# A hybrid attention block: the scan's second operand in PSUM, and dilated queries copied by residue

## The chip, the cores and the metric

The kernel runs on one core of one Trainium2 chip. A core has five engines that run side by side: TensorE (PE, matrix products; its weight loads are shown as PEld), VectorE (DVE), ScalarE (ACT), GpSimd (POOL) and SyncE (SP), which here issues the DMAs. PE reads its operands from SBUF and writes to PSUM, which has eight banks of 128 x 512 floats. Each engine works through its own queue in order and waits on semaphores for the others. The metric is the device time of one execution in microseconds (us), the median of the runs.

## The reference

One layer of a decoder, sequence 1024, width 1024, everything float32. The heads fall into two groups of eight (64 wide). Group A ("dilated") uses normalised, rotated q and k and a softmax over a strided window for three window and stride pairs; group B ("stick-breaking") has no softmax. Cut to what matters here:

```python
DILATED_PAIRS = ((128, 1), (512, 4), (2048, 16))   # (window, dilation)

# group A: every query t attends t, t-r, t-2r, ..., t-window for each (window, r);
# the three results are weighted by their softmax denominators

# group B, one block of 128 queries against all keys, strictly causal
z = jnp.einsum('bhqd,bhkd->bhqk', qblk, k) * scale
log_beta = jax.nn.log_sigmoid(z)
log_keep = jnp.where(causal, jax.nn.log_sigmoid(-z), 0.0)
suffix = lax.cumsum(log_keep, axis=3, reverse=True) - log_keep
a = jnp.where(causal, jnp.exp(log_beta + suffix), 0.0)
out = jnp.einsum('bhqk,bhkd->bhqd', a, v)

# then
mixed = concat(rmsnorm(o_A), rmsnorm(o_B))
x = x + mixed @ w_out
x = x + (silu(h @ w_gate) * (h @ w_up)) @ w_down,  h = rmsnorm(x)
```

## The kernel before

The program is straight-line code; a scheduler puts the instructions of each engine in an order from a simulated timeline, and allots the buffers of each tag in the order in which the program asks for them. Products are exact to float32 by splitting one or both factors into a high and a low part, so most products are two or three matmuls (`mm3`).

The stages, in order: the norm of x and the projection of v for group A; q and k for group A with norm and rotation (`rope_norm`), written to DRAM; the attention of the eight head pairs; the output projection; the feed-forward part, from about 650 us to the end, whose products follow a seven-product scheme (lines 884 to 1110). The change concerns the attention.

A *pair* is two heads, stored one above the other in the 128 partitions. Pairs 0 to 3 are group A, 4 to 7 group B. `prep` gets a pair's operands ready while the pair before it is attended: `set_k` and `set_q` write `kh`, `kl` (high and low part of k) and `qs` (q, high part in one half of the partitions, low part in the other, one tile for each head s). `more()` issues background work between the steps, metered by `LEAD`, `PRE` and `RATES`: the projections of the later pairs (`project`, tile pp), and then `merge_a`, group A's share of the output projection (tile yo). `hold` ties the background matmuls to the score matmul `gate[0]` that stands before them in the program.

Group A, `attend_a` (589): two halves hf of 512 queries, four blocks k in each, and for each block two kinds of unit (`unit_a`, 407). The near unit (lay 0) has 128 neighbouring queries against up to 256 neighbouring keys. The dilated unit (lay 1) has the 128 queries of one residue mod 4 in the half, against the keys of that residue, which `set_k` stores together. Its q is taken by a stride:

```python
if lay:
    n = 128 * hf + 128
    q, keys = slice(512 * hf + k, 512 * hf + 512, 4), lambda t: t[:, 256 * k:256 * k + n]
```

In both kinds q is the matmul's weights (420, 421) and the keys stream past. DVE adds a mask and takes the row's extreme (422), ACT the exponential (424). Some units later `turn_a` (461) turns the result on PE (469), `evac` (502) copies it out, and PE multiplies it by v (478) into an accumulator: near in the PSUM tag "t", dilated in "pv"; ACT copies both out at the end of a half (483). `factors` and `finish` weigh the two kinds, through small DMAs and POOL products (585, 586).

Group B, `attend_b` (611): for each block of 128 queries and each head, `unit_b` (517) makes the scores (401 to 404), ACT two sigmoids into kp and p (522), DVE a running product of kp backward (525), and POOL for one head, DVE for the other, the product of p with it (526). The scan is

```python
nc.vector.tensor_tensor_scan(rv, rv, rv, 1.0, op0=ALU.mult, op1=ALU.bypass)
```

whose second operation is a bypass, so its second input does not count; here it is kp once more. `ptpv` (529) turns the result (542) and multiplies by v (551). Buffers: kp has two (tag "G"), the scores two PSUM banks ("s").

PSUM tags and their banks: "d" 2, "t" 1, "s" 2, "pt" 2, "pv" 1. `out_rstd` (647) makes the output's norm from sums of squares that PE adds up in a small tile ssp: in tag "t", but in "d" for the last one. Its squares are gathered in `acc`, one tile of 128 x 1024 (705, 757). The output tiles reloaded for it (`load_o`, 642) are in tag "qr", as the rotated q and k were before.

Of the kernel before, what the change touches and what calls it, by code (L numbers as in the profile page):

```python
# [11 lines left out]
F32 = mybir.dt.float32  # L12
FR = mybir.dt.float32r
AF = mybir.ActivationFunctionType
ALU = mybir.AluOpType
# [17 lines left out]
def f(ap):  # L33
    return ap.bitcast(F32)
# [3 lines left out]
def tile_hybrid_block(ctx, tc, x, attn_norm_w, w_in, q_norm_w, k_norm_w, dil_w, sb_w,  # L38
# [276 lines left out]
    def set_q(pr, hf, p):  # L315
        sl = slice(hf * 512, hf * 512 + 512)
        for s in range(2):
            a, b = slice(64 * s, 64 * s + 64), slice(64 - 64 * s, 128 - 64 * s)
            nc.scalar.activation(pr.qs[s][a, sl], p[a, :], AF.Copy)
            nc.vector.tensor_tensor(pr.qs[s][b, sl], p[a, :], f(pr.qs[s][a, sl]), op=ALU.subtract)  # L320

    def set_k(pr, hf, p):

        def half(t):
            return t.rearrange("p (c w) -> p c w", c=4)[:, :, 128 * hf:128 * hf + 128]

        p = p.rearrange("p (c w) -> p c w", c=4)
        for s in range(2):
            a, b = slice(64 * s, 64 * s + 64), slice(64 - 64 * s, 128 - 64 * s)
            kh, kl = half(pr.kh[s]), half(pr.kl[s])  # L330
            nc.scalar.activation(kh[a], p[a], AF.Copy)
            nc.scalar.activation(kh[b], p[a], AF.Copy)
            nc.vector.tensor_tensor(kl[a], p[a], f(kh[a]), op=ALU.subtract)
# [24 lines left out]
    def back(qr):  # L358
        p = PS.tile([128, 512], F32, "pt", "bk")
        for k in range(4):  # L360
            nc.tensor.transpose(p[:, k * 128:(k + 1) * 128], qr[:, k, :], ident)
        return p

    def prep(pr, g, i):

        pr.ot, pr.g, pr.i = [None, None], g, i
        head_tiles(pr, i)
        if g == 0:
            for which, put in ((1, set_k), (0, set_q)):
                for hf in range(2):  # L370
                    t = att.tile([128, 4, 128], F32, tag="rl", name="rl", bufs=3)
                    nc.sync.dma_start(t, qk[which][hf * 512:hf * 512 + 512, 128 * i:128 * i + 128].rearrange(("(t p) e -> p t e", "(p t) e -> p t e")[which], t=4))
                    put(pr, hf, back(t))
                    yield 0.9
            for hf in range(2):
                set_va(pr, hf, i)
            yield 0.1
        else:
            todo = [(1, hf, s, 0.3) for hf in range(2) for s in range(2)] + [(which, hf, None, 0.6) for which in (0, 2) for hf in range(2)]
            there = []  # L380
            for n, (which, hf, s, cost) in enumerate(todo):
                while len(there) < min(n + 3, len(todo)):
                    w, h, one, _ = todo[len(there)]
                    while (1, i, w, h) not in ready:
                        more()
                    there.append(load_raw(1, i, w, h, one))
                t = there[n]
                if which == 1:
                    set_kb(pr, hf, s, t)
                else:  # L390
                    (set_q, None, set_v)[which](pr, hf, t)
                yield cost
# [14 lines left out]
    def unit_a(pr, s, lay, k, hf, p, nm, den):  # L407


        if lay:  # L410
            n = 128 * hf + 128
            q, keys = slice(512 * hf + k, 512 * hf + 512, 4), lambda t: t[:, 256 * k:256 * k + n]
        else:
            c = 512 * hf + 128 * k
            n = 256 if c else 128
            q, w = slice(c, c + 128), (c + 128 - n) // 4

            keys = lambda t: t.rearrange("p (c w) -> p c w", c=4)[:, :, w:w + n // 4].rearrange("p c (b u) -> p b c u", u=32)
        sp = PS.tile([128, 512], F32, "s", "sc")[:, :n]
        gate[0] = nc.tensor.matmul(sp, pr.qs[s][:, q], keys(pr.kh[s]), start=True, stop=False)  # L420
        nc.tensor.matmul(sp, pr.qs[s][:, q], keys(pr.kl[s]), start=False, stop=True)  # L421
        nc.vector.tensor_tensor_reduce(p[:, :n], sp, mask[:, lay, 256 - n:256], scale=-0.125, scalar=3.0e38,  # L422
                                       op0=ALU.add, op1=ALU.min, accum_out=nm)
        last_exp[0] = nc.scalar.activation(p[:, :n], p[:, :n], AF.Exp, bias=nm, scale=-1.0, accum_out=den)
# [92 lines left out]
    def unit_b(pr, s, qb, tag):  # L517
        n = (qb + 1) * 128
        p, kp = P4("pb", tag), P4("kp", "G")
        for sp, c0, c1 in scores(pr, s, qb):  # L520
            for t, scale in ((kp, -0.125), (p, 0.125)):
                i = nc.scalar.activation(t[:, c0:c1], sp, AF.Sigmoid, scale=scale)  # L522
                after(i, last_exp[0], "one activation table at a time")
        rv = kp[:, n - 1::-1] if n == 1024 else kp[:, :n][:, ::-1]
        nc.vector.tensor_tensor_scan(rv, rv, rv, 1.0, op0=ALU.mult, op1=ALU.bypass)  # L525
        (nc.gpsimd, nc.vector)[s].tensor_tensor(p[:, :n - 1], p[:, :n - 1], kp[:, 1:n], op=ALU.mult)  # L526
        return p

# [60 lines left out]
    def attend_a(pr, o):  # L589

        pr.acc, pr.o = [None, None], [[None, None], [None, None]]
        for hf in range(2):
            p = []
            st = att.tile([128, 2, 4, 2, 2], F32, tag="st", name="st", bufs=2)
            for k in range(4):
                p.append(P4("pa"))
                for lay in range(2):
                    n = 128 * hf + 128 if lay else 256 if hf or k else 128
                    for s in range(2):
                        c = 512 * lay + 256 * s + (0 if lay else 256 - n)  # L600
                        unit_a(pr, s, lay, k, hf, p[k][:, c:c + n], st[:, lay, k, 0, s:s + 1], st[:, lay, k, 1, s:s + 1])
                    catch_up(2 if len(pend) > 2 else 1)
                    yield 1.5
                for items in far(pr, hf, k) + near(pr, hf, k):
                    pend.append((now[0], lambda items=items, p=p, hf=hf: turn_a(pr, hf, p, items)))
            weigh, wide = factors(st)
            wait = WEIGH + (2 if hf and pr.i == 3 else 0)
            chores.append((now[0] + wait, weigh))
            chores.append((now[0] + wait + USE, lambda hf=hf, wide=wide: finish(pr, hf, o, wide)))

    def attend_b(pr, o):

        late = None
        for g in range(4):
            pq = []
            for k in range(2):
                pq.append([unit_b(pr, s, 2 * g + k, "PPPE"[2 * k + s]) for s in range(2)])
                catch_up(2)
                yield 0.2 * (2 * g + k + 1)
            if late:  # L620
                while pend:
                    catch_up(9)
                ptpv(*late)
                yield 0.92 * (2 * late[1] + 1.5)
            late = (pr, g, pq, o)
        ptpv(*late)
        yield 0.92 * (2 * late[1] + 1.5)
# [18 lines left out]

    def out_rstd(g, hf, acc):

        ssp = PS.tile([128, 4], F32, "d" if g and hf else "t", "ssp")
        for k in range(4):  # L650
            nc.tensor.matmul(ssp[:, k:k + 1], acc[hf][:, k * 128:(k + 1) * 128], ones, start=True, stop=True)
        r = big.tile([128, 4], F32, name="rg%d%d" % (g, hf))
        nc.vector.tensor_scalar(r, ssp, 1.0 / 512, EPS, op0=ALU.mult, op1=ALU.add)
        nc.gpsimd.tensor_tensor(r, r, mhalf[:, :4], op=ALU.pow)
        return r
# [44 lines left out]
    def merge_a():  # L700
        for tt in range(4):
            t = H("x2", F32)
            x2.append(t)
        parts = [[H("oh"), H("ol")] for hf in range(2)]
        t = att.tile([128, 1024], F32, tag="acc", name="acc", bufs=1)
        acc = [t[:, 0:512], t[:, 512:1024]]
        for hf in range(2):
            for tt in (2 * hf, 2 * hf + 1):
                nc.sync.dma_start(x2[tt].rearrange("p (a c) n -> p a (c n)", a=2),
                                  x[tt * 256:(tt + 1) * 256, :].rearrange("(a p) d -> p a d", p=128))  # L710
            yield from merge(0, hf, parts, acc)
# [42 lines left out]
        more()  # L754

    parts = [[H("oh"), H("ol")] for hf in range(2)]
    t = att.tile([128, 1024], F32, tag="acc", name="acc", bufs=1)
    acc = [t[:, 0:512], t[:, 512:1024]]
    for _ in merge(1, 0, parts, acc):
        pass  # L760
    tail = merge(1, 1, parts, acc)
# [256 lines left out]
    sums = [H("tk", F32) for _ in range(4)]  # L1018
    right_sum = [t[:, k, :] for t in sums[:3] for k in range(4)]
    left_sum = [sums[3][:, k, :] for k in range(4)]  # L1020
    for tag, n in (("k2", 2), ("k2", 2), ("acc", 1), ("kh", 4)):
        t = att.tile([128, 1024], F32, tag=tag, name="lk", bufs=n)
        left_sum += [t[:, 0:512], t[:, 512:1024]]

# [129 lines left out]
```

## Time and profile before

| | us |
|---|---|
| median of 3 runs | 1328.32 |
| lowest, highest | 1328.2, 1330.47 |
| the profiled execution's own time | 1330.71 |
| its span (first to last instruction) | 1328.9 |

The mean granted clock of TensorE was 0.986 of full speed in the profiled execution. How to read its rows: a row of the line view has the line in the code, the engine, the operation, the tile written and those read, how often, and then the durations in ns (least, median, most). A row of the groups has busy time in us, the mean of one in ns and the idle time of the engine in front of it with what ended it. A row of the timeline has start and length in us; matmuls are pipelined, so their lengths overlap, and the distance from start to start tells what one costs. A row of the waits has the sum in us, how often, and the longest. A row of the windows has from and to, the length, busy time and instructions of PE, PEld, DVE, ACT and POOL, then the granted clock, the share of time that the DMA engines were busy, and GB/s. The chain is the row of instructions that ended last, each held up by the one before it.

### The profile page before, as it was taken

The numbers are of one execution on the slowest core, as the hardware profiler recorded it, in microseconds if no ns is written. First come the engines' busy times: TensorE is split into PE (matmuls) and PEld (weight loads), VectorE is DVE, ScalarE is ACT, GpSimd is POOL, SyncE is SP. The second block draws the span as 40 slices with busy tenths as digits, with TensorE's granted clock in tenths as the row PEclk, the third lists the DMA queues.
The fourth block names the chain that finished last, engine by engine and source line by source line (L and its number), as shares of the span: only waits on it lengthen the run. The fifth ranks groups of instructions, "written<-read, shape, count | busy, mean of one in ns | idle before, by whom it ended". The sixth has DMA issues, their size and how long they took to land.

```text
span 1328.9 us, 18238 instructions
## 1 busy us (share of the span) xinstructions
PE 1286.0 (97%) x6260; PEld 1019.1 (77%) x6260; DVE 857.2 (65%) x1407; ACT 624.1 (47%) x1305; POOL 387.3 (29%) x318
## 2 busy tenths in 40 slices
PE   7999999999978978999999999999999999999998
PEld 6888887777756755767888888888888887788886
DVE  4224345556478767794779677666546777985775
ACT  6331266776676867664555222233332323344442
POOL 6388701211224325243312222222222321010000
PEclk9999999999989999999999999999999999999999
DMA  9533133554323143122326654422546448502642
GB/s 279 208 111 103 72 113 104 127 139 114 107 86 113 61 154 135 56 79 81 103 68 213 187 167 135 142 88 79 151 136 198 122 150 302 165 30 97 197 137 86
DMA packets 189324, 172.58 MB, mean 130 GB/s; under 512 B 33712, under 2 KB 134192, under 8 KB 189232
## 3 DMA queue, kind: packets, MB, share of 16 engines
q1 hardware_dynamic: 189232, 171.42, 41.6%
q8 instruction: 49, 0.80, 0.3%
q14 instruction: 43, 0.35, 0.1%
HBM read 133.96 MB, written 37.42 MB: 129 GB/s over the span
## 4 chain that ended last, share of the span: by engine, by line
PE 85%; DVE 4%; ACT 4%; DMA 4%; issue 2%; POOL 1%; SPq 0%; DVEq 0%; ACTq 0%; POOLq 0%
PE yd L1054 14%; PE gu L94 11%; PE gu L95 11%; PE gu L91 11%; PE va L95 3%; PE va L91 3%; PE va L94 3%; PE pp L91 3%; PE pp L94 3%; PE pp L95 3%; PE pv L551 2%; PE yo L94 2%; PE yo L91 2%; PE yo L95 2%; PE pv L478 2%
## 5 line engine op out<-in xcount | busy, mean ns | idle before, releaser
L829 ACT ACTIVATE wh<-wr 128x512 fp32r<-128x512 f32 x132 | 83.2, 631 | 209.1 <-PE gu L94 163.2
L94 PE MATMUL gu<-t,wh 128*128 128x512 f32 x352 | 139.0, 395 | 0.0
L91 PE MATMUL gu<-t,wh 128*128 128x512 f32 x352 | 138.8, 394 | 0.0
L95 PE MATMUL gu<-t,wl 128*128 128x512 f32 x352 | 138.8, 394 | 0.0
L525 DVE TENSOR_TENSOR_SCAN kp<-kp 128x128 f32<-128x128 f32 (+7 forms) x64 | 108.5, 1706 | 28.1 <-ACT kp L522 26.4
L1054 PE MATMUL yd<-dl,dh 128*128 128x512 f32 x308 | 122.4, 397 | 3.1 <-DVE dl L830 2.9
L1054 PE MATMUL yd<-dh,dl 128*128 128x512 f32 x308 | 121.6, 395 | 0.0
L94 PE MATMUL gu<-b,wh 128*128 128x512 f32 x264 | 104.5, 396 | 0.0
L91 PE MATMUL gu<-b,wh 128*128 128x512 f32 x264 | 104.3, 396 | 0.0
L95 PE MATMUL gu<-b,wl 128*128 128x512 f32 x264 | 104.2, 396 | 0.0
L830 DVE TENSOR_TENSOR wl<-wr,wh 128x512 fp32r<-128x512 f32 x105 | 80.6, 767 | 7.8 <-ACT wh L829 7.7
L1054 PE MATMUL yd<-dh 128*128 128x512 f32 x308 | 85.5, 398 | 0.0
L526 POOL TENSOR_TENSOR pb<-pb,kp 128x127 f32<-128x127 f32 (+7 forms) x32 | 43.0, 1345 | 128.5 <-DVE kp L525 54.7
L422 DVE CUSTOM_DVE_ANT_0 pa<-sc,mask 128x256 f32<-128x256 f32 (+1 forms) x128 | 46.3, 380 | 50.6 <-PE sc L421 49.6
L95 PE MATMUL va<-wt,hl 128*128 128x512 f32 x192 | 76.4, 401 | 2.6 <-DVE hl L62 2.6
L91 PE MATMUL va<-wt,hh 128*128 128x512 f32 x192 | 76.6, 405 | 1.9 <-ACT hh L61 1.9
L91 PEld LDWEIGHTS gu<-t,wh 128*128 128x128 f32 x352 | 66.2, 188 | 15.8
L91 PE MATMUL pp<-hh,wh 128*128 128x512 f32 x192 | 78.2, 408 | 0.0
L94 PEld LDWEIGHTS gu<-t,wh 128*128 128x128 f32 x352 | 66.2, 188 | 15.7
L95 PEld LDWEIGHTS gu<-t,wl 128*128 128x128 f32 x352 | 66.1, 188 | 15.6
L829 ACT ACTIVATE dh<-wd 128x512 fp32r<-128x512 f32 x55 | 34.8, 632 | 91.3 <-PE yd L1054 84.5
L94 PE MATMUL va<-wt,hh 128*128 128x512 f32 x192 | 76.4, 400 | 0.0
(208 smaller groups left out, 3166.0 us busy)
## 6 DMA issues: line engine op xcount, KB each, us to landing
wd<-in_w_down_dram SPq DMA_DIRECT2D x88, 256.0 KB, 2.8
wr<-in_w_gate_dram SPq DMA_DIRECT2D x80, 256.0 KB, 3.0
wr<-in_w_up_dram SPq DMA_DIRECT2D x60, 256.0 KB, 3.1
raw<-in_w_in_dram SPq DMA_DIRECT2D x48, 256.0 KB, 4.0
raw<-in_w_out_dram SPq DMA_DIRECT2D x32, 256.0 KB, 2.9
raw<-rq SPq DMA_DIRECT2D x24, 256.0 KB, 2.5
g<-gu SPq DMA_DIRECT2D x20, 256.0 KB, 5.9
xt<-in_x_dram SPq DMA_DIRECT2D x8, 512.0 KB, 6.9
```

What stands on the lines that cost most here:

```text
L91: i = nc.tensor.matmul(ps, a[0], b[0], start=first, stop=False)
L94: nc.tensor.matmul(ps, a[0], b[1], start=False, stop=False)
L95: return nc.tensor.matmul(ps, a[1], b[0], start=False, stop=last)
L422: nc.vector.tensor_tensor_reduce(p[:, :n], sp, mask[:, lay, 256 - n:256], scale=-0.125, scalar=3.0e38, op0=ALU.add, op1=ALU.min, accum_out=nm)
L478: nc.tensor.matmul(pr.acc[lay][64 * s:64 * s + 64, cols], v[:, 64 * s:64 * s + 64], th[:, c:c + n], start=first, stop=last)
L525: nc.vector.tensor_tensor_scan(rv, rv, rv, 1.0, op0=ALU.mult, op1=ALU.bypass)
L526: (nc.gpsimd, nc.vector)[s].tensor_tensor(p[:, :n - 1], p[:, :n - 1], kp[:, 1:n], op=ALU.mult)
L551: i = nc.tensor.matmul(pr.pv[64 * s:64 * s + 64, c - n:c], pr.v[:, j, 64 * s:64 * s + 64], th[:, n * s:n * s + n], start=j == 0, stop=j == ...
L829: nc.scalar.activation(h, r, AF.Copy)
L830: two(n).tensor_tensor(l, r, f(h), op=ALU.subtract)
L1054: mm = nc.tensor.matmul(pp[k], a[x][:, c], b[y], start=not more and j == 0 and x + y == 0, stop=j == HF - 1 and x == 1, skip_group_check=True)
```

## The change

Two edits and what they need. First, `by_residue` copies each half of q on POOL into a tile qf in which the four residues stand one after another, and the dilated unit takes a contiguous block of it as weights. The first half is copied in `prep`, the second at the start of `attend_a`. The tiles are in tags "acc" (head 0) and "qr" (head 1), two buffers each; `acc` becomes two tiles of 512 columns for that. Second, the scan's bypassed input becomes one column of zeros in PSUM, spread over all columns by a step of zero. It lies in the one bank of tag "t" for the whole of group B, so that the sums of squares (ssp) move from "t" to "d".

```diff
+    def by_residue(pr, hf):
+
+        for s in range(2):
+            t = att.tile([128, 512], FR, tag=("acc", "qr")[s], name="qf", bufs=2)
+            nc.gpsimd.tensor_copy(t.rearrange("p (c w) -> p c w", c=4), f(pr.qs[s][:, hf * 512:hf * 512 + 512]).rearrange("p (w c) -> p c w", c=4))
+            pr.qf[hf].append(t)
...
     def prep(pr, g, i):
-        pr.ot, pr.g, pr.i = [None, None], g, i
+        pr.ot, pr.g, pr.i, pr.qf = [None, None], g, i, [[], []]
...
                     put(pr, hf, back(t))
+                    if which == 0 and hf == 0:
+                        by_residue(pr, 0)
                     yield 0.9
...
         if lay:
             n = 128 * hf + 128
-            q, keys = slice(512 * hf + k, 512 * hf + 512, 4), lambda t: t[:, 256 * k:256 * k + n]
+            q, keys = pr.qf[hf][s][:, 128 * k:128 * k + 128], lambda t: t[:, 256 * k:256 * k + n]
         else:
...
-            q, w = slice(c, c + 128), (c + 128 - n) // 4
+            q, w = pr.qs[s][:, c:c + 128], (c + 128 - n) // 4
...
-        gate[0] = nc.tensor.matmul(sp, pr.qs[s][:, q], keys(pr.kh[s]), start=True, stop=False)
-        nc.tensor.matmul(sp, pr.qs[s][:, q], keys(pr.kl[s]), start=False, stop=True)
+        gate[0] = nc.tensor.matmul(sp, q, keys(pr.kh[s]), start=True, stop=False)
+        nc.tensor.matmul(sp, q, keys(pr.kl[s]), start=False, stop=True)
...
-        nc.vector.tensor_tensor_scan(rv, rv, rv, 1.0, op0=ALU.mult, op1=ALU.bypass)
+        nc.vector.tensor_tensor_scan(rv, rv, aside[0][:, 0:1].to_broadcast([128, n]), 1.0, op0=ALU.mult, op1=ALU.bypass)
...
     def attend_a(pr, o):
         pr.acc, pr.o = [None, None], [[None, None], [None, None]]
+        by_residue(pr, 1)
...
+    aside = [None]
     def attend_b(pr, o):
+        if aside[0] is None:
+            aside[0] = PS.tile([128, 512], F32, "t", "aside")
+            nc.vector.memset(aside[0][:, 0:1], 0.0)
...
     def out_rstd(g, hf, acc):
-        ssp = PS.tile([128, 4], F32, "d" if g and hf else "t", "ssp")
+        ssp = PS.tile([128, 4], F32, "d", "ssp")
...
-    t = att.tile([128, 1024], F32, tag="acc", name="acc", bufs=1)
-    acc = [t[:, 0:512], t[:, 512:1024]]
+    acc = [att.tile([128, 512], F32, tag="acc", name="acc", bufs=2) for _ in range(2)]
...
+    left_sum += [att.tile([128, 512], F32, tag="acc", name="lk", bufs=2) for _ in range(2)]
-    for tag, n in (("k2", 2), ("k2", 2), ("acc", 1), ("kh", 4)):
+    for tag, n in (("k2", 2), ("k2", 2), ("kh", 4)):
```

More of the change, by code (lines that the diff above doesn't have):

```diff
@@ L756, in tile_hybrid_block @@
     parts = [[H("oh"), H("ol")] for hf in range(2)]
-    t = att.tile([128, 1024], F32, tag="acc", name="acc", bufs=1)
-    acc = [t[:, 0:512], t[:, 512:1024]]
+    acc = [att.tile([128, 512], F32, tag="acc", name="acc", bufs=2) for _ in range(2)]
     for _ in merge(1, 0, parts, acc):
```

## The prediction

> **What bounds the kernel now.** I read the page first, then the windows by stage, then the PE timeline inside the dilated stage, then the waits and the chain inside the stick-breaking stage. The page gives the span:
>
> ```profile
> span 1328.9 us, 18238 instructions
> ```
>
> The change touches two stages only: the dilated attention (lines 420 to 424, about 176 to 363 us) and the stick-breaking attention (lines 401 to 526, about 363 to 590 us). The windows view, with PE, PEld, DVE, ACT and POOL busy time and then the granted clock:
>
> ```profile
> 176.00:363.00 187.00, 186.23 (x1162) 146.88 (x1161) 99.12 (x387) 131.87 (x382) 35.99 (x28) 1.00 0.43 114
> 363.00:590.00 227.00, 200.02 (x1154) 146.97 (x1153) 176.15 (x155) 161.34 (x353) 84.73 (x53) 0.94 0.29 93
> ```
>
> The reader sees two different limits. In the first stage PE is busy 186.23 of 187 us at full clock: anything that PE stops doing there shortens the stage until ACT (131.87) is the next limit. In the second PE is idle for 227 − 200.0 = 27 us, its clock falls to 0.94, and DVE is busy 176 us: something in the DVE, ACT and POOL chain holds PE up at times, but DVE too is idle for 51 us, so it isn't a plain DVE bound.
>
> **Part 1: q as contiguous weights.** The line view of L420 and four pairs of rows from the PE timeline. Each pair is the first matmul of four (two heads, each against kh and kl) and a background matmul behind it:
>
> ```profile
> L420 PEld LDWEIGHTS sc<-kh,qs x128: 186/250/334, 177.4 to 359.6; 128*128 128x128 f32 x128
> ```
>
> ```profile
> 256.83 0.48 PE L420 MATMUL sc<-kh,qs 128*128 128x256 f32 x1
> ...
> 257.85 0.40 PE L91 MATMUL pp<-hh,wh 128*128 128x512 f32 x1
> ...
> 260.33 0.36 PE L420 MATMUL sc<-kh,qs 128*128 128x256 f32 x1
> ...
> 260.89 0.40 PE L91 MATMUL pp<-hh,wh 128*128 128x512 f32 x1
> ```
>
> ```profile
> 226.34 0.23 PE L420 MATMUL sc<-kh,qs 128*128 128x128 f32 x1
> ...
> 227.38 0.39 PE L94 MATMUL pp<-hl,wh 128*128 128x512 f32 x1
> ...
> 177.60 0.22 PE L420 MATMUL sc<-kh,qs 128*128 128x128 f32 x1
> ...
> 178.28 0.40 PE L94 MATMUL pp<-hl,wh 128*128 128x512 f32 x1
> ```
>
> The weight loads come in two kinds, 186 to 334 ns. Units alternate between near (contiguous q) and dilated (every fourth q). With 256 keys, the slow four take 257.85 − 256.83 = 1.02 us and the fast four 260.89 − 260.33 = 0.56: 0.46 apart, for equal moving sizes. With 128 keys I measure to the second background matmul, because the slow load delays the first one as well: 227.38 − 226.34 = 1.04 against 178.28 − 177.60 = 0.68, 0.36 apart. The keys of the slow units are the contiguous ones, so it is the strided q as weights that costs.
>
> L420 runs 128 times: 64 near, 64 dilated, that is 32 dilated fours, 16 with 128 keys and 16 with 256. Sum: 16 × 0.46 + 16 × 0.36 = **13.1 us** of PE time, in a stage where PE has 0.8 us to spare. The most would be 32 × 0.46 = 14.7. The least is 0, if another chain takes its place; ACT has 55 us idle there and DVE 88, and the scores are turned and multiplied several units later, so I take all of it.
>
> The Trainium skill, "SBUF — State Buffer", section "Door 1: The DMA port swizzle", in its note on 16-byte cachelines, says that accesses that each cross to a new line pay, yet also that fp32 may be strided by 4 for free. Its second half speaks against this edit, since q's step is 4 floats; by it the sum would lose the 13.1 and leave about 1322. The loads of 334 beside 186 ns side with the first half.
>
> What it adds: 16 POOL copies (4 pairs × 2 halves × 2 heads) of 128x512 with a strided read. No such copy is in the trace; the nearest rows are
>
> ```profile
> L308 POOL MEMSET kl<- 64x1024 f32 x4 | 3.7, 946 | 12.2 <-PE ptr L109 12.2
> L665 POOL TENSOR_TENSOR wo<-raw,wo 128x512 fp32r<-128x512 f32 x16 | 27.2, 1709 | 20.0 <-ACT wo L664 12.9 <-issue 6.8
> ```
>
> a write of 1024 columns and a contended two-input operation of the same size. So 0.5 to 1.7 us; I take 1.2, between them, some 19 us on a POOL that is busy 36 of 187. Cover: the first half is copied a pair ahead, the second at the pair's start, eight half-steps (some 20 us) before its first reader. Only the first pair is short of it, worth 1 to 2 us at most, and background projections are queued there. In POOL's queue nothing behind a copy is urgent, and a copy sits behind no wait long enough to use up the slack. I cost it at 0; without the cover it is two copies, 2.4 us, per half. No DMA is added or moved. That qf shares the tags of acc and of the reloaded outputs holds back loads and squares that now run early, with a whole stage to spare: 0.
>
> **Part 2: the scans.** The page's group of all 64 scans, two scans with nothing beside them, and a POOL product:
>
> ```profile
> L525 DVE TENSOR_TENSOR_SCAN kp<-kp 128x128 f32<-128x128 f32 (+7 forms) x64 | 108.5, 1706 | 28.1 <-ACT kp L522 26.4
> ```
>
> ```profile
> 364.21 0.42 DVE L525 TENSOR_TENSOR_SCAN kp<-kp 128x128 f32<-128x128 f32 x1 [1.15 <-ACT kp L522]
> 571.75 2.02 DVE L525 TENSOR_TENSOR_SCAN kp<-kp 128x896 f32<-128x896 f32 x1
> 509.41 1.54 POOL L526 TENSOR_TENSOR pb<-pb,kp 128x767 f32<-128x767 f32 x1 [8.57 <-DVE kp L525]
> ```
>
> From 0.42 at 128 columns and 2.02 at 896 a scan costs 0.153 + 2.083 ns a column. Eight sizes (128 to 1024), eight of each, are 36,864 columns: 76.8 + 64 × 0.153 = 86.6 us. Measured are 108.5, so 21.9 us aren't the scan's own. The next rows tell where they are; first the chain, then the same scans with their sizes:
>
> ```profile
> 509.93 2.65 DVE kp L525
> 519.33 3.11 DVE kp L525
> 566.52 3.13 DVE kp L525
> 583.63 4.08 DVE kp L525
> ```
>
> ```profile
> 509.93 2.64 DVE L525 TENSOR_TENSOR_SCAN kp<-kp 128x768 f32<-128x768 f32 x1 [0.69 <-ACT kp L522]
> 519.33 3.10 DVE L525 TENSOR_TENSOR_SCAN kp<-kp 128x896 f32<-128x896 f32 x1
> 566.52 3.13 DVE L525 TENSOR_TENSOR_SCAN kp<-kp 128x768 f32<-128x768 f32 x1 [0.20 <-ACT kp L522]
> 583.63 4.08 DVE L525 TENSOR_TENSOR_SCAN kp<-kp 128x1024 f32<-128x1024 f32 x1
> ```
>
> The second head's scan starts while POOL multiplies the first head's. The scan at 509.93 finds POOL at work from 509.41 to 510.95, 1.02 us more, and takes 2.64 where its own time is 1.75: 0.89 longer. It all but waits POOL out. Would an operand in PSUM avoid it? Two rows of plain operations of 512 columns:
>
> ```profile
> L865 DVE TENSOR_TENSOR u<-gu,u 128x512 f32<-128x512 f32 x54 | 37.0, 685 | 21.2 <-PE gu L95 20.2 <-DMA u<-early 0.9
> L830 DVE TENSOR_TENSOR t<-t,t 128x512 fp32r<-128x512 f32 x16 | 10.9, 680 | 0.0
> ```
>
> With a PSUM operand 685 ns, with both in SBUF and POOL out of the way 680. So PSUM costs nothing per column and I take 86.6 for the scans. The Trainium skill, "SBUF — State Buffer", section "Who interferes with whom", says a Vector instruction with two SBUF inputs and a GpSimd one that reads SBUF lock each other out for a whole instruction, and with one SBUF input don't; by it the sum is the same 21.9, and the stretched scans agree.
>
> How much reaches the end? Scans on the chain: 0.89 + 1.09 + 1.37 + (4.08 − 2.28) = **5.2 us** that go with the lock. PE's idle 27 us also lower its clock: 0.06 × 227 = 13.6 us lost, of which 5.2/27 comes back, 2.6. Together **7.8**. Least 0 (the rest of the chain, exponentials and DMA, is late next), most 21.9 + 13.6, held by the 27 + 13.6 that PE has to give. The waits say why I stay low; of PE's two longest only the second is the scans' own:
>
> ```profile
> PE sc L401 <- ACT pb L522: 7.8, 7, 3.8
> PE pt L542 <- DVE pb L526: 6.5, 7, 1.5
> ACT qs L319 <- DMA rl<-raw: 11.4, 3, 4.4
> ```
>
> **Part 3: the PSUM bank.** The operand is a column of bank "t", which also holds the near accumulator of the dilated stage. Its memset, and so the first scan, must wait for that accumulator's last copy:
>
> ```profile
> 369.22 0.63 ACT L338 ACTIVATE kh<-rl 128x512 fp32r<-128x512 f32 x1 [3.55 <-DMA rl<-raw]
> ...
> 375.12 0.61 ACT L483 ACTIVATE o<-pv 128x512 f32<-128x512 f32 x1
> ```
>
> The first scan moves from 364.21 to about 375.8, 11.5 us. Behind it wait POOL's and DVE's products, then the sigmoids of the next block, as kp has two buffers, and the scores behind them. But ACT, in whose queue the second block's sigmoids stand, waited for a DMA until 369.22, so that block was late as it is, and without its sigmoids in front the copy comes sooner. So 0 to 11.5; I take **+2**, nearer the small end, as that stall hides most of it. The norm sums that leave "t" for "d" (two buffers): each takes a "d" buffer for one small DVE read while one product fills the other, 0.
>
> **Sum.** −13.1 − 7.8 + 2 = −18.9. The profiled execution took 1330.7 us, 1.8 around its span; it becomes 1311.8. It lies 2.4 above the median of the runs, so the median becomes 1328.3 − 18.9 = **1309**. Its own range is 1300 to 1317.
>
> **The rivals.**
> - **The second stage gives nothing back**: the bank's wait costs up to 11 and the freed DVE time waits for DMA and ACT. For it: the 11.4 us that ACT waits for q's loads; against it: the locked scans on the chain. 1328.3 − 13.1 + 0 to 6: 1315 to 1322. Chance 0.18.
> - **The second stage is freed wholly**: 21.9 of scans and most of the clock: 1328.3 − 13.1 − 13 to 27, 1288 to 1302. For it: DVE is its busiest helper; against: the first wait row, whose longest piece is a DMA's. Chance 0.12.
> - **Part 1 doesn't do what it says**: stride isn't what slows the load, or ACT becomes late at once. Then −7.8 + 2: 1322. Against it: 186 and 334 ns alternate with the units. Chance 0.05.
> - **Slower**: the scan reads PSUM by a slower path, at 3 cycles a column and not 2. That adds 36,864 × 1.04 = 38.4: scans of 125.0, 16.5 above now, all on the path at worst: −13.1 + 2 + 16.5, 1334. It turns slower from a mean scan of (108.5 + 11.1)/64 = 1.87 us. Against it: 685 beside 680 ns. Chance 0.05.
>
> **How the numbers follow.** The forecast has 0.57; the last 0.03 is no visible change. Faster by over 0.2% (about what a measurement of this kernel can tell from none, 2.7 us): 0.57 + 0.18 + 0.12 + 0.05, cut to 0.90 for the overlap with the bank's cost; same 0.05; slower 0.05. The range runs from the middle of the second rival to the end of the first, 1296 to 1322.
>
> **What would show it.** Right: all L420 loads near 190 ns, dilated fours of 0.56 us, the first stage near 174 us with PE still full; 64 scans at 86 to 88 us whatever POOL does; the first scan some 10 us behind the first sigmoid; the second stage 4 to 8 us shorter. Wrong: dilated matmuls that wait for POOL's qf, scans above 1.4 us in the mean, or a new idle stretch of PE between the stages that is longer than 6 us.

## The result and the profile after

The median went from 1328.26 us (1326.69 to 1330.47) to 1310.05 us (1308.62 to 1310.73), 18.2 us less. The measured ratio, which is not the quotient of these medians (0.9863), is 0.9853 [0.9839, 0.9867], or 19.5 us less. The profiled execution of the changed kernel took 1310.01 us; its span is 20.7 us shorter than that of before. The mean granted clock rose from 0.986 to 0.990. First the page of the changed kernel:

```profile
span 1308.2 us, 18283 instructions
```

Then its windows: group A's stage, cut 12 us earlier than before, as group B's first scores come 12.4 us earlier; the 220 us behind it; and the 30 us around the seam between them. After the three columns of time come PE, PEld, DVE, ACT and POOL, then the granted clock, DMA share and GB/s:

```profile
176.00:351.00 175.00, 172.36 (x1163) 131.93 (x1162) 101.21 (x386) 128.74 (x380) 50.08 (x40) 1.00 0.45 118
351.00:571.00 220.00, 195.19 (x1157) 143.41 (x1156) 160.64 (x162) 162.98 (x359) 69.29 (x53) 0.96 0.32 103
346.00:376.00 30.00, 20.18 (x118) 14.94 (x117) 18.86 (x30) 17.85 (x41) 8.40 (x8) 0.77 0.42 117
```

PE is still nearly full in group A's stage, but 2.6 us are idle where 0.8 were. In group B PE is idle for 24.8 of 220 us, where it was 27 of 227, at a clock of 0.96 in place of 0.94. Of that idle time 9.8 us lie in the third row, at the seam, where PE's clock was 0.77.

The view of one line, the scores of group A, shows the weight loads (PEld) and what they waited for:

```profile
L429 PEld LDWEIGHTS sc<-kh,qs x64: 186/188/192, 177.0 to 345.1; 128*128 128x128 f32 x64
...
L429 PEld LDWEIGHTS sc<-kh,qf x64: 186/190/217, 180.1 to 347.5; 128*128 128x128 f32 x64
...
  POOL qf L326: 1.0, 1
```

The two kinds of load have become one. The copies were waited for once, for 1.0 us. The page's group of the scans:

```profile
L534 DVE TENSOR_TENSOR_SCAN kp<-kp,aside 128x128 f32<-128x128 f32 (+7 forms) x64 | 85.4, 1347 | 29.2 <-ACT kp L531 28.9
```

108.5 us have become 85.4, where 86.6 were worked out as the scans' own time. The timeline of one microsecond shows a scan beside POOL's product:

```profile
393.04 1.78 POOL L535 TENSOR_TENSOR pb<-pb,kp 128x895 f32<-128x895 f32 x1 [6.48 <-PE pt L551]
...
393.51 2.02 DVE L534 TENSOR_TENSOR_SCAN kp<-kp,aside 128x896 f32<-128x896 f32 x1 [0.64 <-ACT kp L531]
```

POOL works until 394.82, so for 1.31 us of the scan's 2.02, and 2.02 us is what 896 columns took before with nothing beside them.

**Where the time came from.** Three stretches can be cut out of the two stages by the first and last matmuls of three lines. For group B the rows are, of the kernel before and then of the changed one:

```profile
L401 PE MATMUL sc<-kh,qs x96: 220/446/775, 361.6 to 579.3; 128*128 128x512 f32 x48, 128*128 128x128 f32 x16, 128*128 128x256 f32 x16, 128*128 128x384 f32 x16
...
L551 PE MATMUL pv<-th,v x320: 272/379/688, 381.7 to 613.1; 128*64 128x256 f32 x128, 128*64 128x128 f32 x32
```

```profile
L410 PE MATMUL sc<-kh,qs x96: 220/442/775, 349.2 to 558.6; 128*128 128x512 f32 x48, 128*128 128x128 f32 x16, 128*128 128x256 f32 x16, 128*128 128x384 f32 x16
...
L560 PE MATMUL pv<-th,v x320: 272/379/689, 374.6 to 591.5; 128*64 128x256 f32 x128, 128*64 128x128 f32 x32
```

"A" is the time from group A's first score to its last, "start of B" from group B's first score to its first product with v, "rest of B" from there to the last score. In us, for the profiled execution of each kernel that is spoken of below:

| kernel | A | start of B | rest of B |
|---|---|---|---|
| before | 182.1 | 361.6 to 381.7: 20.1 | to 579.3: 197.6 |
| after | 170.3 | 349.2 to 374.6: 25.4 | to 558.6: 184.0 |
| after, once more on another chip | 170.4 | 25.3 | 187.1 |
| part 1 alone | 172.7 | 25.4 | 195.5 |
| part 2 alone | 184.1 | 22.2 | 185.8 |
| copies made but not read | 182.8 | 21.5 | 196.9 |
| bank taken later | 170.7 | 23.5 | 183.7 |
| scan with a zero in SBUF | 170.9 | 24.4 | 193.4 |
| loads later | 173.1 | 16.2 | 193.8 |
| loads and bank later | 171.0 | 13.2 | 192.4 |

The change gained 11.8 us in A and 13.6 in the rest of B, and gave back 5.3 at the start of B. The second profile of the same kernel has 3.1 us more in the rest of B, and the kernel whose copies nobody reads has 1.4 more at the start than the kernel before: differences of this size between single profiles carry no meaning. Background work that PE does sooner or later can shift time between the last two columns as well.

### The profile page after: what moved, and what is told of

It reads as the page before. It is cut to its first block, busy times and chain, and to the rows that moved or that the text cites. A ratio compares the mean times of both kernels' runs of the same rounds, so it can differ in the third digit from the quotient of the medians.

```text
span 1308.2 us, 18283 instructions
## 1 busy us (share of the span) xinstructions
PE 1264.8 (97%) x6260; PEld 998.6 (76%) x6260; DVE 839.7 (64%) x1408; ACT 621.4 (47%) x1305; POOL 390.3 (30%) x334
## 4 chain that ended last, share of the span: by engine, by line
PE 87%; DMA 4%; ACT 3%; DVE 3%; issue 2%; SPq 0%; POOL 0%; DVEq 0%; ACTq 0%; POOLq 0%
PE yd L1069 14%; PE gu L94 11%; PE gu L95 11%; PE gu L91 11%; PE va L95 3%; PE va L91 3%; PE va L94 3%; PE pp L91 3%; PE pp L94 3%; PE pp L95 3%; PE pv L560 2%; PE yo L91 2%; PE pv L487 2%; PE yo L95 2%; PE yo L94 2%; PE pt L551 2%
## 5 line engine op out<-in xcount | busy, mean ns | idle before, releaser
L534 DVE TENSOR_TENSOR_SCAN kp<-kp,aside 128x128 f32<-128x128 f32 (+7 forms) x64 | 85.4, 1347 | 29.2 <-ACT kp L531 28.9
L95 PE MATMUL pp<-hh,wl 128*128 128x512 f32 x192 | 76.0, 396 | 0.0
L94 PE MATMUL pp<-hl,wh 128*128 128x512 f32 x192 | 75.6, 394 | 0.0
```

The lines of the kernel that those rows point to most:

```text
L94: nc.tensor.matmul(ps, a[0], b[1], start=False, stop=False)
L95: return nc.tensor.matmul(ps, a[1], b[0], start=False, stop=last)
L534: nc.vector.tensor_tensor_scan(rv, rv, aside[0][:, 0:1].to_broadcast([128, n]), 1.0, op0=ALU.mult, op1=ALU.bypass)
```

## The experiments

Ratios are against the kernel before on the same chip, whose median there was 1331 to 1332 us; "x us" is one minus the ratio, times 1328.3. Here too a ratio need not be the quotient of the medians: for part 2 alone that would be 0.9929, or 9.5 us less, beside 0.9941.

**Each part alone.** The first kernel has the copies and nothing of the scan's edit; the second is the kernel before with the scan's edit.

```diff
 # part 1 alone
-        nc.vector.tensor_tensor_scan(rv, rv, aside[0][:, 0:1].to_broadcast([128, n]), 1.0, op0=ALU.mult, op1=ALU.bypass)
+        nc.vector.tensor_tensor_scan(rv, rv, rv, 1.0, op0=ALU.mult, op1=ALU.bypass)
 # part 2 alone
-            q, keys = pr.qf[hf][s][:, 128 * k:128 * k + 128], lambda t: t[:, 256 * k:256 * k + n]
+            q, keys = slice(512 * hf + k, 512 * hf + 512, 4), lambda t: t[:, 256 * k:256 * k + n]
```

> Only the contiguous copy of q; the scans read kp twice as before, no bank is held, and ssp is back in tag t. The theory of the prediction: 13.1 us less than before, 1315 us, with all dilated weight loads near 190 ns, scans at 108 us in sum, and the first scan about 4 us behind the first sigmoid or earlier. By the trace of the changed kernel, in which the last dilated unit came 12 us earlier: 1316. The rival that the dilated stage only moves the waits into the next stage (the DMA loads at the seam of the stages don't get shorter): 1320 to 1325.

> Only the scan's second input in PSUM, with the bank held from the start of group B and ssp in tag d; q is strided as before. By the prediction's terms -7.8 + 2: 1322.5 us. By the trace of the changed kernel, where group B is about 14 us shorter behind its start and its start about 5 us longer: -9, 1319. Both expect scans of 85 to 87 us in sum. The rival that the two parts need each other (the scans' gain shows only when PE is freed before): 1326 to 1330.

Part 1 alone: 1321.49 us, 0.9919 [0.9893, 0.9945], 10.8 us less. Part 2 alone: 1322.27 us, 0.9941 [0.9924, 0.9958], 7.8 us less. Together that is 18.6, and the change as a whole took off 17.9 to 19.5 (0.9865 [0.9849, 0.9881] on another chip, 0.9853 above): the parts add up. The table says where each acts. Part 1 takes 9.4 us out of A and puts 5.3 into the start of B, where no bank was held: that loss belongs to part 1, and with it part 1 lands where the rival of its expectation stood (1320 to 1325), not at 1315. Part 2 takes 11.8 us out of the rest of B and puts 2.1 into its start. The groups of the scans, of part 1 alone and of part 2 alone:

```profile
L534 DVE TENSOR_TENSOR_SCAN kp<-kp 128x128 f32<-128x128 f32 (+7 forms) x64 | 108.9, 1712 | 28.5 <-ACT kp L531 26.8
```

```profile
L525 DVE TENSOR_TENSOR_SCAN kp<-kp,aside 128x128 f32<-128x128 f32 (+7 forms) x64 | 85.4, 1348 | 30.6 <-ACT kp L522 30.5
```

**The copies alone.** Part 1 has a cost (POOL's copies, the shared buffers) and a gain (contiguous weights). This kernel makes the copies and doesn't read them.

```diff
-            q, keys = pr.qf[hf][s][:, 128 * k:128 * k + 128], lambda t: t[:, 256 * k:256 * k + n]
+            q, keys = pr.qs[s][:, 512 * hf + k:512 * hf + 512:4], lambda t: t[:, 256 * k:256 * k + n]
...
-        nc.vector.tensor_tensor_scan(rv, rv, aside[0][:, 0:1].to_broadcast([128, n]), 1.0, op0=ALU.mult, op1=ALU.bypass)
+        nc.vector.tensor_tensor_scan(rv, rv, rv, 1.0, op0=ALU.mult, op1=ALU.bypass)
```

> The kernel before with the 16 POOL copies of q by residue and their tiles, which nothing reads: the units take their strided q and the scans read kp twice. It prices what part 1 adds. The prediction costs the copies at 0: within 2 us of the kernel before. The rival that the copies cost on their way (POOL's queue, POOL's reads against DVE, the tags of acc and of the reloaded outputs): 3 to 6 us slower, which would be the difference between the 13 us predicted for part 1 and the 8 to 11 measured.

1331.05 us, 0.9997 [0.9987, 1.0007]. The copies are there, 18.3 us of POOL by the line view, and cost nothing that shows:

```profile
L326 POOL CAST qf<-qs 128x512 fp32r<-128x512 f32 x16 | 18.3, 1148 | 35.3 <-DVE qs L320 35.0 <-POOL qf L326 0.3
```

**A step of two floats.** The copy keeps two residues side by side, so that the weights have a step of 8 bytes in place of 16 (before) or 4 (after).

```diff
-            nc.gpsimd.tensor_copy(t.rearrange("p (c w) -> p c w", c=4), f(pr.qs[s][:, hf * 512:hf * 512 + 512]).rearrange("p (w c) -> p c w", c=4))
+            nc.gpsimd.tensor_copy(t.rearrange("p (d w c) -> p d w c", d=2, c=2), f(pr.qs[s][:, hf * 512:hf * 512 + 512]).rearrange("p (w d c) -> p d w c", d=2, c=2))
...
-            q, keys = pr.qf[hf][s][:, 128 * k:128 * k + 128], lambda t: t[:, 256 * k:256 * k + n]
+            q, keys = pr.qf[hf][s][:, 256 * (k // 2) + k % 2:256 * (k // 2) + 256:2], lambda t: t[:, 256 * k:256 * k + n]
```

> The changed kernel, but the copy keeps two residues side by side, so that the dilated weights have a step of 2 floats (8 bytes) in place of 1; before it was 4 (16 bytes). If what counts is whether two reads fall into one 16-byte piece: loads near 190 ns and 1310 us. If every step above 1 costs: loads between 190 and 334 ns and up to 13 us more.

The view of line 429, and the line view's group of the copies:

```profile
L429 PEld LDWEIGHTS sc<-kh,qf x64: 192/197/337, 181.2 to 352.1; 128*128 128x128 f32 x64
```

```profile
L326 POOL CAST qf<-qs 128x512 fp32r<-128x512 f32 x16 | 11.2, 707 | 32.5 <-DVE qs L320 29.8 <-PE sc L430 1.7 <-POOL qf L326 0.8
```

The median load is 197 ns, near the 188 of contiguous weights and far from the slow kind, 0.31 to 0.33 us: of the steps tried here, 8 bytes cost next to nothing and 16 bytes do. Of the 128 loads of this line and the next, two are above 250 ns, both where the granted clock was 0.66. The copies became shorter, 707 ns for the 1148 above. The one execution took 1319.79 us, where 1310 was expected; PE's granted clock was 0.66 in it from 316 to 326 us, which nothing here ties to the edit, so its time isn't read.

**A second operand in SBUF that isn't kp.** Is the slow scan one that reads kp twice, or one that has two operands in SBUF? Here the bypassed input is a column of zeros in SBUF, and no bank is taken.

```diff
-        nc.vector.tensor_tensor_scan(rv, rv, aside[0][:, 0:1].to_broadcast([128, n]), 1.0, op0=ALU.mult, op1=ALU.bypass)
+        nc.vector.tensor_tensor_scan(rv, rv, zero.to_broadcast([128, n]), 1.0, op0=ALU.mult, op1=ALU.bypass)
```

> The changed kernel, but the scan's bypassed input is a column of zeros in SBUF, spread by a step of zero, and no bank is held. If it is POOL's reads that lengthen a scan with two inputs in SBUF: scans of 105 to 109 us in sum, long ones beside a POOL product, 1314 to 1317 us as the kernel with the copy of q alone. The rival that the scan is slow because it reads the tile it overwrites a second time: scans of 86 us and a time of 1305 to 1308, for want of a bank's wait.

1324.81 us, 0.9953 [0.9935, 0.9971], above the 1314 to 1317 expected; its ten runs lie between 1321.24 and 1334.25, and part 1 alone, at 0.9919, isn't told from it. The group of its scans:

```profile
L534 DVE TENSOR_TENSOR_SCAN kp<-kp,zero 128x128 f32<-128x128 f32 (+7 forms) x64 | 107.6, 1692 | 27.4 <-ACT kp L531 25.5
```

107.6 us, as before the change: one address, read over and over for a result that doesn't use it, is enough, if it lies in SBUF. What counts is where the operand lies, not that kp is read twice.

**POOL's product taken away.** In the kernel before, DVE multiplies for both heads.

```diff
-        (nc.gpsimd, nc.vector)[s].tensor_tensor(p[:, :n - 1], p[:, :n - 1], kp[:, 1:n], op=ALU.mult)
+        nc.vector.tensor_tensor(p[:, :n - 1], p[:, :n - 1], kp[:, 1:n], op=ALU.mult)
```

> The kernel before, but the products of p with the scanned kp are all on DVE, so that POOL no longer works beside the second head's scan; the scans still have both inputs in SBUF. If POOL's work lengthens them: most of the 22 us goes, scans of 88 to 96 us in sum (POOL's other products, of weights and of the group-A outputs, still fall beside some), with some 30 us more products on DVE. If a scan with both inputs in SBUF is slow by itself: 105 to 109 us again.

The scans with two operands in SBUF, by the page's groups:

```profile
L525 DVE TENSOR_TENSOR_SCAN kp<-kp 128x128 f32<-128x128 f32 (+7 forms) x64 | 91.7, 1437 | 22.3 <-ACT kp L522 22.0
```

16.8 of the 21.9 us are gone with POOL's product. The timeline tells where the rest is, if each scan is set against its own time, 0.153 us + 2.083 ns a column, as worked out in the prediction. The 51 scans that have no POOL work beside them are 0.1 us above it in sum, the 13 others 5.3 us. These 5.3 us lie on scans that found POOL already at work, on the sums of squares (640) or on the low part of the output weights (665). A scan that came first kept its own time, though POOL then worked on the weights (74) or weighed an output (585). One of each, 384 columns behind POOL and 896 columns ahead of it:

```profile
551.18 1.45 POOL L665 TENSOR_TENSOR wo<-raw,wo 128x512 fp32r<-128x512 f32 x1 [0.24 <-ACT wo L664]
551.42 2.02 DVE L525 TENSOR_TENSOR_SCAN kp<-kp 128x384 f32<-128x384 f32 x1
...
401.70 2.02 DVE L525 TENSOR_TENSOR_SCAN kp<-kp 128x896 f32<-128x896 f32 x1
402.22 2.56 POOL L74 TENSOR_TENSOR wl<-raw,wh 128x512 fp32r<-128x512 f32 x1 [24.47 <-ACT wh L72]
```

The first took 2.02 us where its own time is 0.95. By the same count for the kernel before, 23 scans found POOL already at work and are 22.5 us above their own time in sum. The 41 others, with POOL idle or starting behind them, are 0.4 us below theirs. In the changed kernel 23 scans found POOL at work too, and none is longer than its own time. The one execution took 1326.74 us beside 1331.15 of the kernel before, with 32 products more for DVE; a single run says no more than that.

**The bank taken later.** The first four scans (two blocks of two heads) read kp twice as before, and the bank is taken ahead of the third block.

```diff
-        if aside[0] is None:
-            aside[0] = PS.tile([128, 512], F32, "t", "aside")
-            nc.vector.memset(aside[0][:, 0:1], 0.0)
...
+            if g and aside[0] is None:
+                aside[0] = PS.tile([128, 512], F32, "t", "aside")
+                nc.vector.memset(aside[0][:, 0:1], 0.0)
...
+        other = aside[0][:, 0:1].to_broadcast([128, n]) if aside[0] is not None else rv
```

> The changed kernel, but the first four scans of group B (blocks 0 and 1 of its first pair) read kp twice as before, and the bank is taken for the later ones only. If the wait for the bank costs the 5 us by which the start of group B grew: 1305 us, and the first scan within 4 us of the first sigmoid. If it costs the 2 of the prediction: 1308. The rival that the start is held by the DMA loads of the next pair, whatever the scans do: 1310 as the changed kernel.

1310.58 us, 0.9859 [0.9835, 0.9884]: no different from the change. The first scan runs at 352.75, not at 366.34, and yet the start of B is 23.5 us long. First the ACT timeline of the changed kernel, then the ACT and PE timeline of this one:

```profile
359.74 0.63 ACT L345 ACTIVATE kh<-rl 128x512 fp32r<-128x512 f32 x1 [6.26 <-DMA rl<-raw]
360.27 0.58 ACT L515 ACTIVATE th<-pt 128x512 f32<-128x512 f32 x1
...
364.83 0.60 ACT L492 ACTIVATE o<-pv 128x512 f32<-128x512 f32 x1
367.28 0.38 ACT L531 ACTIVATE kp<-sc 128x256 f32<-128x256 f32 x1 [1.85 <-POOL pb L535]
```

```profile
359.92 0.63 ACT L345 ACTIVATE kh<-rl 128x512 fp32r<-128x512 f32 x1 [5.71 <-DMA rl<-raw]
360.46 0.37 ACT L531 ACTIVATE kp<-sc 128x256 f32<-128x256 f32 x1
...
361.15 0.69 PE L410 MATMUL sc<-kh,qs 128*128 128x384 f32 x1 [4.63 <-ACT pb L531]
```

ACT stands at line 345, the next pair's k, until its DMA has landed at 359.7, and everything queued behind it stands too: in the changed kernel the copy of the turned weights (515), for which PE waits, and then the accumulator's copy (492), for which the memset of the bank waits (it ran at 366.25, when DVE was done with the low part of the next pair's q); here the next sigmoids (531). The bank's wait lies behind the DMA's.

**The DMA's wait taken away, then both.** The loads of that pair (the second of group B) are issued behind the first blocks of group B, and the background work that asks for them is metered to begin 2.5 steps later; in the second kernel the bank is taken later as well.

```diff
+            if (g, i) == (1, 1):
+                after(ld, gate[0], "behind the start of group B")
...
-            while fill < FILL[g] * done / 24.0:
+            while fill < FILL[g] * (done if n != 4 else (done - 2.5) * 24 / 21.5) / 24.0:
```

> The changed kernel once more, on the same chip as the next two, for comparison: 0.985 of the kernel before.

> The changed kernel, but the loads of the second group-B pair's operands stand behind the first pair's first blocks, so that ACT's queue holds no work that waits for them at the seam of the stages. If those waits (6.3 us of ACT at the seam in the changed kernel, 3.6 before) ate part of what the contiguous q gave: 3 to 5 us less than the changed kernel, and no PE wait of 5 us for the turned tile's copy. The rival that PE is short of work there whatever ACT waits for: the same time, with the idle stretch elsewhere; the loads then come late for the second pair and cost it as much.

> The later loads together with the later bank (first four scans reading kp twice). With ACT's wait gone the bank's wait is bare: if the first scan waits for the near accumulator's last copy, this is 2 to 4 us below the kernel with the later loads alone. If the bank costs nothing of its own: the same as that kernel.

The change itself, beside them on the same chip: 1312.78 us, 0.9865 [0.9849, 0.9881]. Loads later: 1313.56 us, 0.9865 [0.9847, 0.9883], no gain, where 3 to 5 us were expected if those waits were the cause. Loads and bank later: 1307.76 us, 0.9826 [0.9805, 0.9847], about 5 us below the other two; the intervals touch at 0.9847 to 0.9849. The windows of the seam and of the 44 us behind it, for loads later and then for both later:

```profile
346.00:376.00 30.00, 26.98 (x180) 20.41 (x180) 17.25 (x30) 21.55 (x54) 9.37 (x9) 0.94 0.49 132
376.00:420.00 44.00, 36.45 (x187) 27.77 (x183) 32.64 (x39) 32.07 (x66) 12.45 (x9) 0.84 0.38 114
```

```profile
346.00:376.00 30.00, 28.46 (x188) 21.24 (x187) 22.53 (x36) 25.50 (x61) 11.26 (x10) 1.00 0.45 128
376.00:420.00 44.00, 36.00 (x198) 27.02 (x197) 29.75 (x37) 30.79 (x65) 12.05 (x9) 0.88 0.38 108
```

and the second stretch of the changed kernel:

```profile
376.00:420.00 44.00, 40.12 (x242) 29.80 (x242) 34.53 (x38) 35.58 (x77) 14.62 (x10) 1.00 0.35 103
```

At the seam PE is busy 26.98 us with later loads, in place of 20.18. But in the stretch behind it PE is busy 36.45 of 44 us at a clock of 0.84, where the changed kernel had 40.12 at 1.00 (on this chip 40.37 at 0.92). Part of the difference is background work done earlier, at the seam. Another part shows in the waits of that stretch in the kernel with later loads (total, how often, longest):

```profile
ACT kh L345 <- DMA rl<-raw: 7.8, 4, 2.3
PE pt L551 <- ACT th L553: 3.7, 1, 3.7
```

ACT waited 4.1 us for loads at that line there in the changed kernel, and PE 1.2 us for that copy. The loads that were moved are waited for at their new place, and ACT's queue passes it on to PE again, so the wait was at least in part moved and not removed. That profile is of the slowest of the four executions, 1316.44 us. With the bank later too, ACT's wait in that stretch is still there (8.6 us), but the start of B is 13.2 us, not 16.2, PE's clock at the seam stays at 1.00, and a gain is left. How much of it each wait holds, these runs don't say.

**One load more.** To that kernel, the last one adds that the broadcast of the next norm's weight, which stands ahead of those loads in SP's queue, is issued behind the attention.

```diff
-    nc.sync.dma_start(nw, ffn_norm_w.partition_broadcast(128))
+    i = nc.sync.dma_start(nw, ffn_norm_w.partition_broadcast(128))
+    after(i, gate[0], "behind the attention")
```

> The kernel with the later loads and the later bank, in which the broadcast of the second norm's weights (512 KB) is put behind the attention too; it was issued at the seam of the stages, in front of the loads. If the loads at the seam are slowed by it: 2 to 3 us below the kernel with both, 0.980 to 0.981 of the kernel before. If not: 0.9826 as that kernel, or more, as the norm may then wait for its weights.

1307.44 us, 0.9819 [0.9805, 0.9834]: not to be told from 0.9826. Both are below the change as it was made (0.9853 and 0.9865), by some 4 to 6 us, and below the kernel before by 23 to 24.

## Why the prediction was right, and where its terms were not

The forecast was 1309, and 1310 was measured. The mechanisms were right. That the sum came within 1 us is luck in part: two misses of opposite sign made it nearer than its terms.

**Part 1, contiguous weights: mechanism right, one term too small and one left out.** Loads near 190 ns, fours of 256 keys at 0.56 us, a stage near 174 us with PE nearly full: as said. The term 16 × 0.36 for the units of 128 keys was taken from a four that was of the rarer kind. The PE timeline of before, and then of after, with the second background matmul again as the mark:

```profile
180.48 0.42 PE L420 MATMUL sc<-kh,qs 128*128 128x128 f32 x1
...
181.72 0.39 PE L94 MATMUL pp<-hl,wh 128*128 128x512 f32 x1
```

```profile
228.48 0.31 PE L429 MATMUL sc<-kh,qf 128*128 128x128 f32 x1
...
229.24 0.39 PE L94 MATMUL pp<-hl,wh 128*128 128x512 f32 x1
```

1.24 us became 0.76, 0.48 less. Of the 13 such fours whose background follows at once in the trace of before, 10 took 1.24 to 1.27 and 3 took 1.04. So PE was given (10 × 0.48 + 3 × 0.36)/13 × 16 = 7.2 and 16 × 0.46 = 7.4, some 14.6 us. "I take all of it" failed by 2.6 us: one stretch of group A is not full any more, as the window of the changed kernel shows, where before PE was busy 20.00 of these 20 us.

```profile
300.00:320.00 20.00, 17.36 (x116) 12.50 (x116) 15.26 (x45) 12.97 (x37) 7.78 (x6) 1.00 0.46 137
```

PE waits there for DVE's extremes (line 431) and for ACT's copy of the turned weights (515), up to 1 us at a time, though both have idle time in the stretch as a whole (DVE is busy 15.26, ACT 12.97 us). 14.6 − 2.6 = 12.0, and A became 11.8 shorter. What the step left out is the seam: PE comes to group B 12.4 us earlier (first score 361.6 to 349.2), but ACT can begin on the next pair's k, for whose DMA it waits, only 9.5 us earlier (369.22 to 359.74). ACT's wait there grew from 3.55 to 6.26 us, and the start of B by 5.3; with those loads moved it is 16.2 us. So part 1 alone is worth 10.8, not 13.1.

**The copies at nothing: right.** 1.15 us each (1.2 was taken), one wait of 1.0 us, and 0.9997 where they are made but not read. The cover named, a pair's lead and eight half-steps, was enough.

**Part 2, the scans: mechanism right, its share of the path too small.** 85.4 us for 86.6. That it is the second operand in SBUF together with POOL is shown by two runs, 107.6 us with a column of zeros in SBUF and 91.7 without POOL's product, and by the count of single scans above. The Trainium skill, "SBUF — State Buffer", section "Who interferes with whom", says this of any Vector instruction with two SBUF inputs; both runs agree, also for an input that the operation bypasses. The path's 7.8 (5.2 of scans on the chain and 2.6 of clock) was too little: the rest of B became 11.8 us shorter with part 2 alone, and 11.5 shorter from part 1 alone to the whole change (195.5 to 184.0; 8.4 by the second profile's 187.1). The chain counts only what was last; a scan that ends sooner also lets POOL and DVE begin their products sooner where another wait was nearly as late. That reason is argued, not shown: no run measures those shares apart. These 8 to 12 us lie between the 7.8 and the small end of the rival "freed wholly", 13.

**Part 3, the bank: its reason right, its size within the scatter.** +2 was taken because ACT's stall at the DMA hides the bank's wait. Part 2 alone, which has the bank, has a start of B 2.1 us longer, where the kernel with the unread copies and no bank has 1.4; in the whole change the start is 25.4 us, as in part 1 alone without the bank. Taking the bank later gains nothing as long as ACT waits for the DMA, and some 5 us (3 of them at the start of B) once it doesn't. The first scan came 13.8 us behind the first sigmoid (352.54 to 366.34), where some 10 were said.

**The clause that stood against it.** "A new idle stretch of PE between the stages that is longer than 6 us" was to show the prediction wrong. None is that long; there are two, of 4.96 and 3.49 us, where the longest before was one of 3.83, and they are the loss at the seam. The PE timeline of the changed kernel:

```profile
360.90 2.08 PE L487 MATMUL pv<-th,v 128*64 128x256 f32 x12 [4.96 <-ACT th L515]
...
367.30 0.47 PE L551 MATMUL pt<-ident,pb 128*128 128x128 f32 x1 [3.49 <-POOL pb L535]
```

**The sum, by what was measured.** A 11.8 less, start of B 5.3 more, rest of B 13.6 less: 20.1, and the spans differ by 20.7. Against the terms: −13.1 was −11.8, the seam's +5.3 (with the +2 in it) stood in for +2, and −7.8 was −13.6 (−10.5 by the second profile). The seam left out and the scans' share taken too small nearly cancel.

**What stays open.** The same stage A, with the same code, is 170.3 to 173.1 us long in the profiles of the kernels that read the contiguous copies, and the rest of B of the changed kernel is 184.0 and 187.1 in two, so two or three us between single profiles carry no meaning; part 2 is worth 7 to 9 us from part 1 alone to the change (0.9919 to 0.9853 and 0.9865) and 12 to 13 from the kernel with the zero in SBUF (0.9953), and these runs don't say which of the two is nearer.

## What to carry to other kernels

When a stage that PE fills becomes shorter, look at the first DMA that an in-order engine waits for behind it: if that load's own chain doesn't become earlier by as much, the stage behind gives part of the gain back, and a second wait may be hidden behind the first, so that removing either one alone shows nothing. Look at where each operand lies, even one that an operation ignores: here a second input in SBUF made scans wait for GpSimd's products, and one column in PSUM freed them. Price a saving from several instances of each shape, not from one.

## What the runs showed of the hardware

- Weight loads of 128x128 float32 took 188 ns contiguous and 197 with a step of 8 bytes (medians), and 0.31 to 0.33 us with a step of 16. The Trainium skill, "SBUF — State Buffer", section "Door 1: The DMA port swizzle", lets fp32 be strided by 4 for free; for PE's weights that doesn't hold here, while its remark that at least two hits on a 16-byte line are needed for full bandwidth fits all three loads.
- A scan on DVE costs the same with its bypassed input in PSUM and POOL at work as with that input in SBUF and POOL idle (2.02 us for 896 columns in both). With the input in SBUF, even a single zero, 64 scans beside POOL's products took 107.6 us in place of 85.4; only scans that found POOL already at work were longer (25 of them, by 21.6 us in sum).
- The same strided rearrangement on POOL took 1.15 us for 512 columns with single floats, and 0.71 with pairs of them.
